# A hybrid decoder layer: output products in two groups of tiles instead of three, key norms in eight columns, chain copies on ScalarE

## The chip, the cores and the metric

The kernel runs on one core of a Trainium2 chip, in one launch. The metric is device time in microseconds of the whole program. TensorE multiplies, VectorE, ScalarE and GpSimd (POOL in the rows) work element by element, SyncE (SP) issues most DMAs. All data are float32.

## The reference, cut to what matters

```python
x = x + 0.5 * swiglu(rms_norm(x, ffn1_norm), ffn1_w_in, ffn1_w_out)     # half step 1
h = rms_norm(x, mix_norm)
p_rwkv, p_q, p_k, p_v, p_gate = split(h @ w_in)
y_a = rwkv7_time_mix(p_rwkv, ...)      # 16 heads of 64, 1024 tokens
y_b = dilated_attention(p_q, p_k, p_v, ...)
x = x + (sigmoid(gate_a) * (y_a @ w_proj_rwkv) + sigmoid(gate_b) * (y_b @ w_proj_attn)) @ w_out
x = x + 0.5 * swiglu(rms_norm(x, ffn2_norm), ffn2_w_in, ffn2_w_out)     # half step 2

def swiglu(h, w_in, w_out):            # D_FF = 2816 = 22 tiles of 128
    gate, up = split(h @ w_in)
    return (silu(gate) * up) @ w_out

# in rwkv7_time_mix
kk = heads(k * k_k)
kk = kk / maximum(sqrt(sum(kk * kk, axis=-1)), 1e-12)
k = k * (1 + (a - 1) * k_a)
wkv = wkv7_scan(r, decay, k, v, -kk, kk * a)    # state = state*w + (state@a) b + v k, out = state@r
```

x is 1024 tokens by 1024 columns; the output has the same shape.

## The kernel before, in words

Every large product is made at float32 quality from three float32r products: each operand is split into a high part (a cast, ScalarE, L74) and a rest (a subtraction, VectorE or GpSimd, L75), and high x high, high x rest and rest x high are summed in PSUM.

**The half steps** (`Ffn`). The activation has 22 row tiles of 128 (called f tiles; 1024 tokens each). Tiles 20 and 21, the last made, stay on the chip and are multiplied with their rows of `w_out` first (`second`, L365). Tiles 0 to 17 were written to memory (`spill`) and are brought back, each together with its rows of `w_out`, as one "raw" tile of 1 MB (`out_raw`, L380, two DMAs). They are multiplied by `Seven`, a scheme with seven block products in place of eight for a 2x2 split: a pair of f tiles gives the operands, `prep` (L104) splits the two operands of one step and makes sums in place on GpSimd, `step` (L129) issues the 12 products of one step into four PSUM tiles. `kk` is the number of pairs in a group. After the last step of each of the seven products `out_evac` (L399) adds the four PSUM tiles to one or two blocks of x each: ten additions per row of four, 40 in a group. Tiles 18 and 19 (`acts_back`, `out_load`, `out_split`) are fetched in between and multiplied last.

`run` (L426) puts the raw tiles in six slots and six parts of the old activation tile (`fresh`, the tiles hhi and hlo), and six more in the slots when the first group is done. Operands are prepared three steps ahead (`RING`). The two sets of PSUM tiles, `pp` and `po`, are taken in turns.

**The mixing stage** (`Rwkv`). The 1024 tokens of a pair of heads are two units of 512; 16 units run in a staggered way: `prep`, `late`, `solve` and `chain` of four neighbouring units are generators that say at which time they want their next piece (`PT`, `ST`, in units), and `drive` takes the earliest. Dense products of the input projection (L593, `pd`) fill TensorE between them. What the framework then makes of it is the order on each engine.

- `prep` (L817) of a unit squares k (L836), sums the squares over each head by a product with a matrix of ones at split precision (`head_sum`, L808, into PSUM tile `pn`), takes the root (L842), the reciprocal of the 128x512 result (L844), a minimum (L845, GpSimd), and multiplies by k (L861). kk then goes into ta (L868), AL (L873) and BK (L875). r's product with the decays (L859, GpSimd) fills AL's third part.
- `solve` (L953) inverts a triangular matrix by 32x32 products (pt, px) with updates of XX on VectorE between them, and makes the state maps M (L1041 to L1043, VectorE, twelve instructions per unit).
- `chain` (L1045) passes the state through eight chunks: product (L1061), state copy (L1064, ScalarE); after four chunks the outputs are copied to `o` (L1070), alternately by ScalarE and VectorE; then their squares are summed (L1082, L1084).

PSUM tiles tagged `ps` are four, used in turn by all these pieces.

Of the kernel before, what the change touches and what calls it, by code (L numbers as in the profile page):

```python
# [7 lines left out]
F32 = mybir.dt.float32  # L8
# [5 lines left out]
P = 128  # L14
# [67 lines left out]
RING = 3  # L82
H = NT // 2
L, R = slice(0, 512), slice(512, 1024)
GK = 3
NG_OUT = 3
OUT = (0, 1, 5, 2, 4, 3, 6)
MIX = (0, 4, 1, 5, 2, 3, 6)
ADDS = (((1, 0), (1, 3)), ((1, 0),), ((1, 3),), ((1, 3), (-1, 1)), ((1, 3), (-1, 2)), ((1, 1),), ((1, 2),))
# [3 lines left out]
class Seven:  # L93
# [3 lines left out]
    def __init__(self, tc, kk, order, ring, banks, pool_a=(), pool_b=()):  # L97


        self.tc, self.kk, self.order, self.ring, self.banks = tc, kk, order, ring, banks  # L100
        self.pool_a, self.pool_b = pool_a, pool_b
        self.b = []

    def prep(self, j, n, k, lo, hi):  # L104

# [23 lines left out]
    def step(self, n, k, evac):  # L129

        nc, last = self.tc.nc, self.kk - 1
        if k == 0:
            pool, tag = self.banks(n)
            self.po = [pool.tile([P, 512], F32, tag=tag, name=tag, bufs=4) for _ in range(H)]
        ah, al, bh, bl = self.b.pop(0)
        for i, po in enumerate(self.po):
            t = slice(i * P, (i + 1) * P)
            nc.tensor.matmul(po, ah[:, t], bh, start=k == 0, stop=False)  # L138
            nc.tensor.matmul(po, ah[:, t], bl, start=False, stop=False)  # L139
            nc.tensor.matmul(po, al[:, t], bh, start=False, stop=k == last)  # L140
            if k == last:
                evac(self.order[n], i, po)


class Ffn:
# [245 lines left out]
        return [t.rearrange("p a b -> p (a b)") for t in self.ring()] + [bt[:, 0], bt[:, 1]]  # L391

    def out_prep(self, j):
        if j < 7 * GK * NG_OUT:
            g, n, k = j // (7 * GK), j // GK % 7, j % GK
            f = 2 * GK * g + k
            self.seven.prep(j, n, k, self.raws[f], self.raws[f + GK])

    def out_evac(self, p, i, ps):  # L399
        V, x = self.tc.nc.vector, self.x  # L400
# [24 lines left out]

    def run(self, before, done):  # L426

        first = 2 * GK * NG_OUT
        slots = iter(range(6))
        for j in range(len(FIRST), len(ORDER)):  # L430
            f, n = ORDER[j]
            self.product(j)
            self.prep(j + RING)
            if f >= NF - 2:
                if n == 0:
                    self.out_load(f)
                elif n == 1:
                    self.out_split(f)
            if f == NF - 1 and n in (0, 1, 5):
                for k in range(2):  # L440
                    m = next(slots)
                    self.out_raw(m // 2 + GK * (m % 2), self.slot(m, F32))
        hT = self.fresh(F32)
        parts = [t.rearrange("p k (a t) -> p k a t", a=2).rearrange("p (b k) a t -> p b (k a) t", b=4) for t in hT]
        for m in range(6):
            self.out_raw(2 * GK + m // 2 + GK * (m % 2), parts[m // 4][:, m % 4])
        banks = lambda n: ((self.cx.ps_d, "pp"), (self.cx.ps_o, "po"))[n % 2]
        self.seven = Seven(self.tc, GK, OUT, self.out_ring, banks, POOL_A)
        for j in range(RING):
            self.out_prep(j)  # L450
        self.second((NF - 2, NF - 1), None)
        self.turn_sums(self.tc.nc.vector.tensor_sub)
        per = 7 * GK
        for j in range(per * NG_OUT):
            self.seven.step(j // GK % 7, j % GK, self.out_evac)
            self.out_prep(j + RING)
            if j == per:
                for m in range(6):
                    self.out_raw(4 * GK + m // 2 + GK * (m % 2), self.slot(m, F32))
            for n in range(2):  # L460
                if j == per + 4 + 6 * n:
                    self.acts_back(first + n)
# [28 lines left out]
def rwkv_consts(tc, cx, pool, dram, W):  # L491
# [28 lines left out]
    nc.gpsimd.memset(ce[0:64, 0:64], 1.0)  # L520
    nc.gpsimd.memset(ce[64:128, 64:128], 1.0)
    nc.vector.tensor_copy(new("bones_r", [P, P], F32R), ce)

    nc.vector.scalar_tensor_tensor(ce, ce, -1.0 / C, cx.ident, ALU.mult, ALU.add)

# [247 lines left out]
class Rwkv:  # L773
# [43 lines left out]
    def prep(self, n):  # L817
# [16 lines left out]
        k = q.k[:, ts_]  # L834
        sq = new("sq", [P, HS])
        nc.scalar.activation(sq, k, AF.Square, scale=col("k_k"))  # L836
        hi = new("sh", [P, HS], 1, F32R)
        V.tensor_copy(hi, sq)
        pn = cx.ps_s.tile([P, 512], F32, tag="ps", name="pn")
        self.head_sum(pn, (sq, hi))  # L840
        kk = new("kk", [P, HS])
        nc.scalar.activation(kk, pn, AF.Sqrt)  # L842
        yield T + PT[1] + 0.03
        V.reciprocal(kk, kk)  # L844
        G.tensor_scalar(kk, kk, 1e12, None, ALU.min)  # L845
        V.tensor_tensor_scan(tw, K["reset"], tw, 0.0, ALU.mult, ALU.add)
        yield T + PT[2]
        lam = new("lam", [P, HC, C + 1])
# [7 lines left out]
        r = q.r[:, ts_]  # L856

        u.AL = AL = new("AL", [P, HC, 3, C], 2)
        G.tensor_mul(AL[:, :, 2], ch(r), lam[:, :, 1:C + 1])  # L859
        yield T + PT[2] + 0.07  # L860
        V.scalar_tensor_tensor(kk, k, col("k_k"), kk, ALU.mult, ALU.mult)  # L861
        yield T + PT[2] + 0.10
        u.k2 = k2 = new("k2", [P, HS], 2)
        V.tensor_scalar(k2, ta, col("k_a"), col("c1"), ALU.mult, ALU.add)
# [3 lines left out]
        V.tensor_mul(ta, ta, kk)  # L868
        BK = u.BK = new("BK", [P, HC, 2, C])
        tt = PT[3]  # L870
        for b, h in enumerate((E, O)):
            yield T + tt
            V.scalar_tensor_tensor(AL[h, :, b], ch(kk)[h], -1.0, lam[h, :, 0:C], ALU.mult, ALU.mult)  # L873
# [171 lines left out]
    def chain(self, n):  # L1045
# [8 lines left out]
        for c in range(HC):  # L1054
# [10 lines left out]
            if i == 3:  # L1065

                for par, dst in enumerate((E, O)):
                    for e, src in enumerate((O, E)):
                        k = slice(c - 3 + e, c + 1, 2)
                        (V.tensor_copy if e else nc.scalar.copy)(o[dst, k], pc[src, par:4:2, e])  # L1070
            yield n + (c + 1) / 8

        p = n // 2
# [661 lines left out]
```

## Time and profile before

| | |
|---|---|
| time, median of 3 runs | 2981.69 us (2977.22 to 2982.45) |
| the profiled execution's own time | 2981.99 us |
| its span | 2980.3 us |
| TensorE busy | 2807.6 us (94%) |
| VectorE busy | 2121.5 us (71%) |
| ScalarE busy | 1262.5 us (42%) |
| GpSimd busy | 1165.5 us (39%) |
| mean granted TensorE clock | 0.987 of 2.4 GHz |

The span runs from the first to the last instruction that the profiler saw; the time has 1.7 us more around it. A busy share is a mean over stages with different limits. The first half step lies in 0 to 725 us, attention to 1183, the RWKV part to about 2010, the merge to 2300, the second half step to the end.

### The profile page before, as it was taken

How to read it: one execution, taken by the hardware profiler on the slowest of the kernel's cores; microseconds unless marked ns; L12 is line 12 of the kernel's file. 1: busy time of each engine (PE TensorE's matmuls, PEld its weight loads, DVE VectorE, ACT ScalarE, POOL GpSimd, SP SyncE). 2: the span in 40 equal slices, each digit the busy share in tenths (PEclk: the TensorE clock that was granted, in tenths of full speed). 3: DMA queues.
4: the chain of work that ended last, by engine and by line, in shares of the span. 5: the costliest groups of instructions: out<-in, count | busy, mean ns of one | idle time of the engine just before them, and what ended most of it. 6: DMA issues, size and time to landing. Idle time of an engine off the chain costs nothing.

```text
span 2980.3 us, 56827 instructions
## 1 busy us (share of the span) xinstructions
PE 2807.6 (94%) x23406; PEld 2232.7 (75%) x23406; DVE 2121.5 (71%) x2924; ACT 1262.5 (42%) x2418; POOL 1165.5 (39%) x1017
## 2 busy tenths in 40 slices
PE   7999998898999999999999998999878999999899
PEld 5888887677667778787778777877666888887677
DVE  7676678998565764767675767442899766678998
ACT  5332232334556663455545555452335332332332
POOL 3333234663101112443434344315775233334653
PEclk9999999999999999999999999999999999999999
DMA  3222225203431124111121111139320122225201
GB/s 113 72 85 82 82 86 197 99 1 90 138 106 36 31 78 125 53 51 45 45 63 47 47 42 52 48 115 307 117 64 22 64 82 82 85 84 213 106 1 57
DMA packets 252244, 246.72 MB, mean 83 GB/s; under 512 B 26288, under 2 KB 192336, under 8 KB 251984
## 3 DMA queue, kind: packets, MB, share of 16 engines
q1 hardware_dynamic: 250832, 238.89, 24.7%
q8 instruction: 184, 3.01, 0.4%
q10 hardware_dynamic: 1152, 4.19, 0.4%
q14 instruction: 76, 0.62, 0.1%
HBM read 181.03 MB, written 62.01 MB: 82 GB/s over the span
## 4 chain that ended last, share of the span: by engine, by line
PE 69%; DVE 21%; issue 4%; DMA 3%; ACT 2%; SPq 0%; POOL 0%; DVEq 0%; ACTq 0%; POOLq 0%
PE pp L282 25%; PE pd L593 22%; DVE bl L75 2%; DVE ob L75 2%; DVE x L403 2%; PE pp L139 2%; PE pp L140 1%; PE pp L138 1%; PE plm L897 1%; PE pc L1061 1%; PE pt L973 1%; PE pl L760 1%; PE px L984 1%; DVE alo L75 1%; PE pz L1019 1%
## 5 line engine op out<-in xcount | busy, mean ns | idle before, releaser
L593 PE MATMUL pd<-hhi,whi 128*128 128x512 f32 (+1 forms) x1064 | 430.6, 405 | 3.8 <-DVE gb L1584 2.2
L593 PE MATMUL pd<-hlo,whi 128*128 128x512 f32 (+1 forms) x1064 | 433.0, 407 | 0.0
L593 PE MATMUL pd<-hhi,wlo 128*128 128x512 f32 (+1 forms) x1064 | 428.8, 403 | 0.6 <-POOL wlo L574 0.6
L574 POOL TENSOR_TENSOR wlo<-raw,whi 128x1024 fp32r<-128x1024 f32 (+2 forms) x69 | 160.8, 2331 | 454.5 <-ACT whi L573 395.2
L282 PE MATMUL pp<-e,bh 128*128 128x512 f32 x1056 | 335.4, 398 | 3.1 <-ACT bh L74 2.5
L253 POOL TENSOR_TENSOR rg<-ru,rg 128x512 f32<-128x512 f32 x44 | 58.1, 1321 | 584.2 <-DVE bl L75 584.2
L282 PE MATMUL pp<-hhi,bl 128*128 128x512 f32 x704 | 277.1, 394 | 2.3 <-DVE bl L75 2.3
L282 PE MATMUL pp<-hhi,bh 128*128 128x512 f32 x704 | 278.0, 395 | 0.0
L282 PE MATMUL pp<-hlo,bh 128*128 128x512 f32 x704 | 276.5, 393 | 0.0
L74 ACT CAST bh<-rg 128x512 fp32r<-128x512 f32 x176 | 105.3, 620 | 331.9 <-PE pp L282 167.8
L593 PEld LDWEIGHTS pd<-hhi,whi 128*128 128x128 f32 (+1 forms) x1064 | 199.6, 188 | 51.3 <-issue 4.6
L282 PEld LDWEIGHTS pp<-e,bh 128*128 128x128 f32 x1056 | 199.0, 189 | 51.7 <-ACT bh L74 3.3
L593 PEld LDWEIGHTS pd<-hlo,whi 128*128 128x128 f32 (+1 forms) x1064 | 199.6, 188 | 48.4 <-issue 5.0
L593 PEld LDWEIGHTS pd<-hhi,wlo 128*128 128x128 f32 (+1 forms) x1064 | 199.7, 188 | 46.3 <-issue 4.2
L282 PE MATMUL pp<-e,bl 128*128 128x512 f32 x528 | 210.0, 398 | 0.0
L75 DVE TENSOR_TENSOR bl<-rg,bh 128x512 fp32r<-128x512 f32 x176 | 156.6, 890 | 73.3 <-ACT bh L74 73.3
L306 DVE TENSOR_TENSOR sg<-sg,pp 128x512 f32<-128x512 f32 x162 | 110.5, 682 | 102.9 <-PE pp L282 102.8
L282 PEld LDWEIGHTS pp<-hhi,bl 128*128 128x128 f32 x704 | 132.7, 189 | 33.4 <-DVE bl L75 3.1
L282 PEld LDWEIGHTS pp<-hlo,bh 128*128 128x128 f32 x704 | 132.8, 189 | 30.0
L282 PEld LDWEIGHTS pp<-hhi,bh 128*128 128x128 f32 x704 | 132.7, 188 | 29.4
L1064 ACT ACTIVATE SV<-pc,lamC 64x64 f32<-64x64 f32 x240 | 73.8, 308 | 116.7 <-PE pc L1061 114.8
L74 ACT CAST bh<-e 128x512 fp32r<-128x512 f32 x84 | 52.1, 620 | 166.5 <-PE pp L139 98.2
(483 smaller groups left out, 6788.7 us busy)
## 6 DMA issues: line engine op xcount, KB each, us to landing
raw<-in_w_in_dram SPq DMA_DIRECT2D x60, 512.0 KB
rg<-in_ffn_w_in_dram SPq DMA_DIRECT2D x44, 512.0 KB
ru<-in_ffn_w_in_dram SPq DMA_DIRECT2D x44, 512.0 KB
act_d<-spill SPq DMA_DIRECT2D x80, 256.0 KB
e<-act_d SPq DMA_DIRECT2D x24, 512.0 KB
e<-in_ffn_w_out_dram SPq DMA_DIRECT2D x24, 512.0 KB
gt_d<-gate SPq DMA_DIRECT2D x32, 256.0 KB
x<-in_x_dram SPq DMA_DIRECT2D x8, 512.0 KB
```

What stands on the lines that cost most here:

```text
L74: nc.scalar.copy(hi, src)
L75: (eng or nc.vector).tensor_sub(lo, src, f32(hi))
L138: nc.tensor.matmul(po, ah[:, t], bh, start=k == 0, stop=False)
L139: nc.tensor.matmul(po, ah[:, t], bl, start=False, stop=False)
L140: nc.tensor.matmul(po, al[:, t], bh, start=False, stop=k == last)
L253: G.tensor_sub(b11, b12, b11)
L282: nc.tensor.matmul(ps, a[:, k], b[:, k], start=m == 0, stop=m == 11)
L306: add = lambda o, a: V.tensor_add(o, a, ps)
L403: (V.tensor_add if sign > 0 else V.tensor_sub)(q, q, ps)
L574: (nc.gpsimd if self.pool_lo else nc.vector).tensor_sub(wlo[:, :kd, :n], raw[:, :kd, :n], f32(whi[:, :kd, :n]))
L593: nc.tensor.matmul(ps[:n], a[:, k, :n], b[:, k, t], start=i == 0, stop=i == 3 * kd - 1)
L1064: nc.scalar.activation(nxt[h, e], pc[h, i, e], AF.Copy, scale=lam[h, c])
```

## The change

It has four parts. (1) The 18 f tiles of the output product form two groups, of five and of four pairs, instead of three groups of three pairs; the first ten raw tiles go to six slots and four parts of the old activation tile, the next four to its other four parts, the last four to slots that come free while the first group's last product is prepared. PSUM tiles are taken in turns through all products of both groups. (2) The squares of k are summed per head by four products whose stationary operand is the 128x128 block of squares and whose moving operand has two columns (`heads`), so that the norms of 128 tokens by eight columns result; root, maximum and reciprocal work on 128x8; GpSimd spreads the result to 128x512, TensorE transposes it back into a PSUM tile `pk`, and kk's product reads that. (3) r's product is issued later. (4) All copies of the chain's outputs are ScalarE's.

```diff
-GK = 3
-NG_OUT = 3
+GROUPS = (5, 4)
+IN_SEVEN = 2 * sum(GROUPS)
+STEPS = [(g, n, k) for g, kk in enumerate(GROUPS) for n in range(7) for k in range(kk)]
...
         if k == 0:
-            pool, tag = self.banks(n)
+            pool, tag = self.banks(self.done)
+            self.done += 1
...
     def out_prep(self, j):
-        if j < 7 * GK * NG_OUT:
-            g, n, k = j // (7 * GK), j // GK % 7, j % GK
-            f = 2 * GK * g + k
-            self.seven.prep(j, n, k, self.raws[f], self.raws[f + GK])
+        if j < len(STEPS):
+            g, n, k = STEPS[j]
+            lo, hi = self.pair(g, k)
+            self.seven.prep(j, n, k, self.raws[lo], self.raws[hi])
+
+    def pair(self, g, k):
+
+        f = 2 * sum(GROUPS[:g]) + k
+        return f, f + GROUPS[g]
...
-        for m in range(6):
-            self.out_raw(2 * GK + m // 2 + GK * (m % 2), parts[m // 4][:, m % 4])
+        places = iter([parts[m // 4][:, m % 4] for m in range(8)])
+        for f in todo:
+            self.out_raw(f, next(places))
+        todo = iter(order[1])
+        for p in places:
+            self.out_raw(next(todo), p)
...
-        per = 7 * GK
-        for j in range(per * NG_OUT):
-            self.seven.step(j // GK % 7, j % GK, self.out_evac)
+        free = (0, 2, 4, 1)
+        per = 7 * GROUPS[0]
+        for j, (g, n, k) in enumerate(STEPS):
+            self.seven.kk = GROUPS[g]
+            self.seven.step(n, k, self.out_evac)
+
+            m = j + RING - (per - GROUPS[0])
+            if g == 0 and 0 <= m - 1 < len(free):
+                self.out_raw(next(todo), self.slot(free[m - 1], F32))
             self.out_prep(j + RING)
-            if j == per:
-                for m in range(6):
-                    self.out_raw(4 * GK + m // 2 + GK * (m % 2), self.slot(m, F32))
...
+    nc.vector.tensor_copy(new("heads", [P, 2]), ce[:, 0:P:C])
...
         nc.scalar.activation(sq, k, AF.Square, scale=col("k_k"))
-        hi = new("sh", [P, HS], 1, F32R)
-        V.tensor_copy(hi, sq)
+
         pn = cx.ps_s.tile([P, 512], F32, tag="ps", name="pn")
-        self.head_sum(pn, (sq, hi))
+        for c in range(4):
+            nc.tensor.matmul(pn[:, 2 * c:2 * c + 2], sq[:, c * P:(c + 1) * P], K["heads"], start=True, stop=True)
+        nrm = new("nrm", [P, 8])
+        nc.scalar.activation(nrm, pn[:, 0:8], AF.Sqrt)
+        yield T + PT[1] + 0.03
+        V.tensor_scalar(nrm, nrm, 1e-12, None, ALU.max)
+        V.reciprocal(nrm, nrm)
         kk = new("kk", [P, HS])
-        nc.scalar.activation(kk, pn, AF.Sqrt)
-        yield T + PT[1] + 0.03
-        V.reciprocal(kk, kk)
-        G.tensor_scalar(kk, kk, 1e12, None, ALU.min)
+        G.tensor_copy(kk.rearrange("p (a c) -> p a c", c=C), nrm.unsqueeze(2).broadcast_to([P, 8, C]))
...
         u.AL = AL = new("AL", [P, HC, 3, C], 2)
-        G.tensor_mul(AL[:, :, 2], ch(r), lam[:, :, 1:C + 1])
+        pk = cx.ps_s.tile([P, 512], F32, tag="ps", name="pk")
+        for c in range(4):
+            nc.tensor.transpose(pk[:, c * P:(c + 1) * P], kk[:, c * P:(c + 1) * P], cx.ident)
         yield T + PT[2] + 0.07
-        V.scalar_tensor_tensor(kk, k, col("k_k"), kk, ALU.mult, ALU.mult)
+        V.scalar_tensor_tensor(kk, k, col("k_k"), pk, ALU.mult, ALU.mult)
...
         tt = PT[3]
+        yield T + tt
+        G.tensor_mul(AL[:, :, 2], ch(r), lam[:, :, 1:C + 1])
...
-                        (V.tensor_copy if e else nc.scalar.copy)(o[dst, k], pc[src, par:4:2, e])
+                        nc.scalar.copy(o[dst, k], pc[src, par:4:2, e])
```

What it makes of the order, at three places. Line numbers of the changed kernel are its own; behind the change they are up to 24 higher than before.

VectorE in the output product of the first half step, one product's end to the next one's. Before (x are the additions out of PSUM, bl and ob the rests of the two operands of a step):

```order
L403 TENSOR_TENSOR x<-x,pp 128x512 x8
L75 TENSOR_TENSOR bl<-hlo,bh 128x512
L75 TENSOR_TENSOR ob<-hlo,ob 128x512
L75 TENSOR_TENSOR bl<-hhi,bh 128x512
L75 TENSOR_TENSOR ob<-hhi,ob 128x512
L75 TENSOR_TENSOR bl<-hhi,bh 128x512
L75 TENSOR_TENSOR ob<-hhi,ob 128x512
L403 TENSOR_TENSOR x<-x,po 128x512 x4
```

With the change, in the second group:

```order
L411 TENSOR_TENSOR x<-x,po 128x512 x8
L75 TENSOR_TENSOR bl<-e,bh 128x512
L75 TENSOR_TENSOR ob<-e,ob 128x512
L75 TENSOR_TENSOR bl<-e,bh 128x512
L75 TENSOR_TENSOR ob<-e,ob 128x512
L75 TENSOR_TENSOR bl<-hlo,bh 128x512
L75 TENSOR_TENSOR ob<-hlo,ob 128x512
L75 TENSOR_TENSOR bl<-hlo,bh 128x512
L75 TENSOR_TENSOR ob<-hlo,ob 128x512
L411 TENSOR_TENSOR x<-x,pp 128x512 x4
```

Four steps' splits stand between two blocks of additions (five in the first group), where three stood.

SP's queue in the same stage; hlo and e are places of raw tiles (the old activation tile, the slots), vu the loads for tiles 18 and 19. Before:

```order
L384 DMA hlo<-act_d 128x1024
L385 DMA hlo<-in_ffn_w_out_dram 128x1024
L360 DMA vu<-act_d 128x512 x2
L349 DMA vu<-in_ffn_w_out_dram 128x512 x2
L360 DMA vu<-act_d 128x512 x2
L349 DMA vu<-in_ffn_w_out_dram 128x512 x2
L384 DMA e<-act_d 128x1024
L385 DMA e<-in_ffn_w_out_dram 128x1024
```

With the change:

```order
L387 DMA hlo<-act_d 128x1024
L388 DMA hlo<-in_ffn_w_out_dram 128x1024
L387 DMA hlo<-act_d 128x1024
L388 DMA hlo<-in_ffn_w_out_dram 128x1024
L363 DMA vu<-act_d 128x512 x2
L352 DMA vu<-in_ffn_w_out_dram 128x512 x2
L363 DMA vu<-act_d 128x512 x2
L352 DMA vu<-in_ffn_w_out_dram 128x512 x2
L387 DMA e<-act_d 128x1024
L388 DMA e<-in_ffn_w_out_dram 128x1024
```

Four DMAs more stand ahead of vu; the reloads of the slots stay behind it, four tiles instead of six.

VectorE in the unit of the RWKV part that has r's dense product beside it. Before, ahead of the updates of M and behind them:

```order
L844 RECIPROCAL kk<-kk 128x512
L651 SCALAR_TENSOR_TENSOR k<-pd,v_mu,k 128x511
L655 TENSOR_TENSOR k<-k,carry 128x1
L861 SCALAR_TENSOR_TENSOR kk<-k,v_k_k,kk 128x512
L868 TENSOR_TENSOR ta<-ta,kk 128x512
L1070 COPY o<-pc 64x2x64 x2
L1041 TENSOR_TENSOR M<-pm,MB 64x4x128
```

```order
L1043 TENSOR_TENSOR M<-pm,AL 64x4x64
L1084 TENSOR_REDUCE st<-y 128x8
L976 TENSOR_TENSOR B<-pt,mk 128x256
L873 SCALAR_TENSOR_TENSOR AL<-kk,lam 64x8x64
L978 TENSOR_TENSOR XX<-B,eye 128x256
```

With the change, at the same two places:

```order
L862 TENSOR_SCALAR nrm<-nrm 128x8
L863 RECIPROCAL nrm<-nrm 128x8
L669 SCALAR_TENSOR_TENSOR k<-pd,v_mu,k 128x511
L673 TENSOR_TENSOR k<-k,carry 128x1
L1108 TENSOR_REDUCE st<-y 128x8
L1065 TENSOR_TENSOR M<-pm,MB 64x4x128
```

```order
L1067 TENSOR_TENSOR M<-pm,AL 64x4x64
L883 SCALAR_TENSOR_TENSOR kk<-k,v_k_k,pk 128x512
L1000 TENSOR_TENSOR B<-pt,mk 128x256
L890 TENSOR_TENSOR ta<-ta,kk 128x512
L1002 TENSOR_TENSOR XX<-B,eye 128x256
L897 SCALAR_TENSOR_TENSOR AL<-kk,lam 64x8x64
```

The products kk and ta went behind the updates of M, the sum of squares (L1084, now L1108) went ahead of them, and the copies are gone.

## Rows read from the trace of the kernel before

**Rows 1.** The chain that ended last, whole span, by engine.

```profile
PE 69%; DVE 21%; issue 4%; DMA 3%; ACT 2%; SPq 0%; POOL 0%; DVEq 0%; ACTq 0%; POOLq 0%
```

**Rows 2.** Windows: stretch, us; busy (count) PE, PEld, DVE, ACT, POOL; clock, DMA, GB/s.

```profile
503.20:699.80 196.60, 180.77 (x756) 141.37 (x755) 188.27 (x236) 73.41 (x128) 123.81 (x99) 0.99 0.14 42
2756.80:2953.40 196.60, 181.47 (x758) 142.41 (x758) 189.32 (x236) 73.53 (x128) 119.61 (x75) 0.98 0.11 41
2640.00:2690.00 50.00, 50.00 (x218) 40.70 (x217) 35.05 (x43) 14.71 (x26) 17.84 (x12) 1.00 0.28 87
454.00:492.00 38.00, 30.36 (x122) 23.54 (x121) 32.99 (x36) 11.87 (x21) 23.98 (x16) 0.96 0.86 331
```

**Rows 3.** TensorE's waits, 503 to 700 us: us in total, times, longest.

```profile
PE po L139 <- DVE ob L75: 10.8, 10, 3.7
PE pp L139 <- DVE ob L75: 3.2, 4, 1.5
PE pp L138 <- DVE x L403: 1.7, 1, 1.7
```

**Rows 4.** TensorE's waits, 1282 to 1777 us, five pairs of units.

```profile
PE pt L973 <- DVE XX L986: 12.8, 5, 2.6
PE px L984 <- DVE B L976: 10.9, 10, 1.2
```

**Rows 5.** Windows of the roomy and the tight unit of one pair.

```profile
1493.30:1543.20 49.90, 49.80 (x901) 41.15 (x901) 28.86 (x53) 26.71 (x57) 22.22 (x29) 1.00 0.23 66
1543.20:1592.20 49.00, 43.53 (x893) 35.32 (x893) 37.26 (x67) 26.04 (x58) 17.99 (x29) 1.00 0.11 35
```

**Rows 6.** Groups of instructions, VectorE, 505 to 688 us: busy us, mean ns, idle.

```profile
L403 DVE TENSOR_TENSOR x<-x,pp 128x512 f32<-128x512 f32 x68 | 41.5, 675 | 0.0
```

**Rows 7.** Groups of instructions, whole span, VectorE: busy us, mean ns, idle before.

```profile
L844 DVE RECIPROCAL kk<-kk 128x512 f32<-128x512 f32 x16 | 53.6, 3352 | 23.1 <-ACT kk L842 23.1
...
L1070 DVE COPY o<-pc 64x128 f32<-64x128 f32 x64 | 18.2, 284 | 103.0 <-ACT o L1070 102.5
```

**Rows 8.** The chain in 1480 to 1579 us: start, us, what.

```profile
1499.26 0.95 PE pvt L936 x8
...
1508.41 0.44 PE pyt L1093 x4
1508.85 0.39 PE pc L1061 x4
...
1527.81 0.43 PE pn L814
1528.24 0.24 PE pn L815
```

**Rows 9.** VectorE's instructions in order: start, us, what [idle before].

```profile
1512.99 0.69 DVE L951 TENSOR_TENSOR bonus<-pb,v 128x512 f32<-128x512 f32 x1 [2.60 <-PE pb L815]
...
1537.26 0.75 DVE L861 SCALAR_TENSOR_TENSOR kk<-k,v_k_k,kk 128x512 f32<-128x512 f32 x1 [1.47 <-POOL kk L845]
1538.04 0.69 DVE L868 TENSOR_TENSOR ta<-ta,kk 128x512 f32<-128x512 f32 x1
1542.45 0.28 DVE L1070 COPY o<-pc 64x128 f32<-64x128 f32 x1 [3.71 <-ACT o L1070]
...
1543.37 0.69 DVE L1041 TENSOR_TENSOR M<-pm,MB 64x512 f32<-64x512 f32 x1
...
1549.99 0.69 DVE L1084 TENSOR_REDUCE st<-y 128x8 f32<-128x512 f32 x1
...
1568.99 0.28 DVE L1070 COPY o<-pc 64x128 f32<-64x128 f32 x1 [1.95 <-ACT o L1070]
```

**Rows 10.** ScalarE's instructions in order, in the tight unit.

```profile
1543.38 0.63 ACT L1082 ACTIVATE y<-o 128x512 f32<-128x512 f32 x1 [0.35 <-DVE o L1070]
```

**Rows 11.** The chain in 420 to 700 us.

```profile
516.14 0.60 DVE bl L75
...
520.26 1.71 DVE ob L75
```

More of the change, by code (lines that the diff above doesn't have):

```diff
@@ L102, in __init__ @@
         self.b = []
+        self.done = 0
     def prep(self, j, n, k, lo, hi):
@@ L426, in run @@
     def run(self, before, done):
-        first = 2 * GK * NG_OUT
+        first = IN_SEVEN
         slots = iter(range(6))
+        order = [[f for k in range(kk) for f in self.pair(g, k)] for g, kk in enumerate(GROUPS)]
+        todo = iter(order[0])
         for j in range(len(FIRST), len(ORDER)):
@@ L440, in run @@
                 for k in range(2):
-                    m = next(slots)
-                    self.out_raw(m // 2 + GK * (m % 2), self.slot(m, F32))
+                    self.out_raw(next(todo), self.slot(next(slots), F32))
         hT = self.fresh(F32)
         parts = [t.rearrange("p k (a t) -> p k a t", a=2).rearrange("p (b k) a t -> p b (k a) t", b=4) for t in hT]
-        for m in range(6):
-            self.out_raw(2 * GK + m // 2 + GK * (m % 2), parts[m // 4][:, m % 4])
+        places = iter([parts[m // 4][:, m % 4] for m in range(8)])
[4 more added lines that the diff above has]
+            self.out_raw(next(todo), p)
         banks = lambda n: ((self.cx.ps_d, "pp"), (self.cx.ps_o, "po"))[n % 2]
-        self.seven = Seven(self.tc, GK, OUT, self.out_ring, banks, POOL_A)
+        self.seven = Seven(self.tc, GROUPS[0], OUT, self.out_ring, banks, POOL_A)
         for j in range(RING):
```

## The prediction

> **What bounds the kernel now.** I read the whole chain of waits first. TensorE carries most of it and VectorE nearly all the rest [rows 1], so an edit pays only where TensorE stands still, and there the question is what it waits for. So next come the windows of the two stages that the change enters, and TensorE's waits in them.
>
> The first stage is the output product of a feed-forward half step, which stands in the program twice. Both copies last 196.6 us [rows 2]. In a stretch where TensorE never waits, 218 products of 128x512 take 50 us [rows 2], 0.229 us each; the stage's 63 steps have 756 of them, 173.4 us. So 23.2 us of each copy are lost. VectorE is busy 188.3 and 189.3 us of the two [rows 2]: it is the longer engine. TensorE's waits in the first copy, 15.7 us together, all name VectorE [rows 3]: its residual subtractions (L75) and once the additions out of PSUM (L403). The rest of the 23.2 us I put down to products that restart slowly behind a wait; the granted clock is 0.99 there, so little of it is clock.
>
> The second stage is the RWKV part, 16 units. Over five pairs TensorE's solver products wait 23.7 us for VectorE, 4.7 a pair [rows 4]. The two units of a pair are unlike: in one stretch of 49.9 us TensorE is busy 49.8, in the next of 49.0 only 43.5 [rows 5]. I call them the roomy and the tight unit. In the tight one VectorE starts the updates of M at 1543.4 and has no gap before 1567 [rows 9]; that burst is what the solver waits for.
>
> **Fewer groups in the output stage.** Nine pairs of row tiles in two groups (5 and 4) instead of three of 3: the products stay 756, splits and sums per pair stay. What goes is one third of the additions into x: ten per token tile row, four rows, once less, so 40 of 120 additions per copy. One costs 0.675 us alone; in a run 68 of them occupy 41.5 us [rows 6], 0.61 each, so VectorE loses 24.4 us and needs 188.3 - 24.4 = 164 us against TensorE's 173.4. The longest engine becomes TensorE. The order also shows five or four prepared steps between two blocks of additions instead of three, so a block of 8 (4.9 us) has 11 to 13.8 us of products beside it instead of 8.3. Bounds of the gain per copy: 23.2 us if no wait is left; 8 if bunching keeps two thirds of the loss. I take 17, three quarters, since VectorE's demand is 5% under TensorE's but comes in bursts, and eight extra splits still fall in the first group. Two copies: **-34 us**. The banks now alternate across groups too, which removes the wait of 1.7 us for L403 [rows 3]; it is inside the 17.
>
> What could eat this is the loads. Ten tiles of 1 MB must now be there for the first group, four of them in the old activation tile, used from the fourth step. The queues moved 331 GB/s in the stretch that fetches them [rows 2], so two tiles more than before are some 6 us of transfer, and the first steps lie behind the 22 us of products of the last two row tiles: hidden. SP issues four DMAs more ahead of the loads that the spare row tiles wait for; same cover. The last four tiles go to slots that come free when the first group's last product is prepared, seven steps (19 us) before they are read: at that rate 4 MB take 13 us. Cost nothing, with 6 us of cover left.
>
> **Key norms in eight columns.** VectorE loses a reciprocal of 3.35 us per unit [rows 7] and a cast, GpSimd a subtraction; ScalarE's root shrinks. But that reciprocal stands where VectorE waits on both sides of it: right before the tight burst it still waits 3.7 us [rows 9]. So on the path it is worth only what the first unit shows, where nothing runs beside it: **-2 us**. TensorE gives two products (0.43 + 0.24 us on the chain [rows 8]) for four products with a full weight load and two columns, and four transposes. No row has two columns; the nearest with the same weights and type is the state product, two in 0.39 us [rows 8], so four are 0.78 us; above, four of 128 columns take 0.95 [rows 8], below, nothing. Four transposes take 0.44 us [rows 8]. Net 0.78 + 0.44 - 0.67 = +0.55 us a unit (-0.23 to +0.72).
>
> The Trainium skill (TensorE: Matmul & The Clock Gate, Part 4: PE-mode transpose) gives about 275 ns for a transpose of 128x128 within a kernel. By it four would cost 1.1 us, the 16 units 10.6 us more, and the sum below would be 2964; the row here, at float32 and pipelined, says 0.11 each, and I go by the row.
>
> In the roomy units TensorE has no slack, so 8 x 0.55 = **+4.4 us**. In the tight units VectorE decides. There the order moves the product kk and the product ta (0.75 and 0.69 us, before at 1537.3, in a gap [rows 9]) behind the last update of M, because kk now reads the transposes in PSUM. Against that the sum of squares (0.69 us [rows 9]) moves from behind the updates to before them, where it has to wait for ScalarE's copies and square (square at 1543.4 to 1544.0 [rows 10]): the updates start about 1.2 us later. One more PSUM tile per unit in a rotation of four also makes the next solver product wait for the last update instead of the one before it; that shifts TensorE by up to 1.7 us, but into time in which it waits now. Together 0 to +1.2 us a tight unit; I take 0.4, 8 x 0.4 = **+3 us**. Full bounds of the RWKV stage: -44 us (all of 8 x 4.7 gone, no new weight loads, the first unit) to +15 us (8 x 0.72 + 8 x 1.2).
>
> **Copies and r's product.** VectorE gives its two copies of 0.28 us per half unit to ScalarE; they alternate with ScalarE's own, and VectorE waits for each (103 us in all [rows 7]). On ScalarE four in a row end when the fourth ends now. The wait is freed in gaps, in the tight unit the updates wait for TensorE's products until then anyway: nothing. r's product on GpSimd stands later by a sixteenth of a unit; GpSimd sat before it waiting for the last update anyway: nothing.
>
> **The sum.** -34 - 2 + 4.4 + 3 = -28.6. Made against the profiled execution's 2981.99 us (span 2980.3 and 1.7 around it; 0.3 us above the median of the three runs, 2981.69): **2953 us**.
>
> **The rivals.** *The burst dissolves* (10%). VectorE is relieved by some 5 us a unit and TensorE's 4.7 us a pair go: 38 us less, 9 us of new TensorE work, 2 of the first unit: -31 instead of +5, 2917 us. For it: all those waits name VectorE. Against: what is taken off lies outside the burst. *The output stage stays bunched* (10%). A residual subtraction takes 0.60 us alone and 1.7 us when it meets GpSimd [rows 11]; GpSimd's 124 us of work are the same in a shorter stage, so more may be hit. At 1.09 on average the 108 subtractions are 118 us; at 1.25 they are 17 more, which eats most of the 24: gain 5 a copy, 2977 us. The rule behind it is in the Trainium skill (SBUF — State Buffer, SBUF: two separate sides): VectorE with two SBUF inputs and GpSimd exclude each other for a whole instruction. *Slower* (5%): VectorE's queue now waits, at kk, for TensorE's transposes, which wait for a bank that VectorE frees; behind kk stand ta, both halves of AL and BK of the unit, and the solver's first product. If the full sum of the pieces comes on the path in every unit (0.75 + 0.69 + 1.2 + 1.7 = 4.3 us), it costs 69 us and the result is 3015 us. It decides above 2.1 us a unit, where it overtakes the 34. For it: VectorE's burst has no gap; against: in the roomy unit it has one of 2.6 us soon after [rows 9]. *The late reload* (3%), where the change does not do what it says: if the second group's tiles come 10 us late in both copies, 2973 us.
>
> **How the numbers follow.** Forecast 2953 with 72%; its own bounds are 2939 (23 a copy) to 2974 (10 a copy, RWKV +12). Leaving out the dissolved burst and part of the bunched stage, 8 in 10 lie in **2934 to 2974**. What a measurement can tell from no change is 0.2%, 6 us. Faster: the forecast, the dissolved burst, the late reload and a third of the bunched stage, 88%. Same: the rest of that, 7%. Slower: 5%.
>
> **What would show it.** Right: 80 additions instead of 120 in each copy, the copies at 176 to 184 us, TensorE's waits for VectorE there under 6 us; in the RWKV stage a pair of 99 to 101 us with waits of TensorE still 4 to 6 us, now behind an M update or kk; copies only on ScalarE. Wrong: output copies over 190 us, mean subtractions above 1.2 us, GpSimd or ScalarE waiting for a load in the second group's first steps; or pairs under 97 or over 103 us.

## The result, and the profile after

| | before | changed |
|---|---|---|
| time, median | 2981.53 us (4 runs, 2977.22 to 2982.45) | 2997.43 us (4 runs, 2996.12 to 3003.26) |
| ratio | | 1.0062, 95% interval 1.005 to 1.0074 |
| the profiled execution: time, span | 2981.99, 2980.3 us | 3003.26, 3001.5 us |
| TensorE busy | 2807.6 us | 2841.4 us |
| VectorE busy | 2121.5 us | 2002.8 us |
| mean granted TensorE clock | 0.987 | 0.981 |

The change is slower by 0.62%, 15.9 us; the forecast was 2953, with a range of 2934 to 2974. VectorE lost 119 us of work, and TensorE got 34 us more. (The profiled execution is the slowest of the four; the ledger further down is made from one at the median.)

**The output copies.** Windows of the two copies of the changed kernel (columns as in [rows 2]):

```profile
500.90:692.60 191.70, 181.07 (x757) 143.03 (x755) 169.43 (x204) 72.70 (x128) 122.28 (x99) 0.98 0.12 34
2783.80:2974.50 190.70, 179.71 (x757) 143.19 (x756) 169.37 (x197) 72.73 (x128) 117.15 (x75) 0.98 0.09 31
```

They were 196.6 us [rows 2] and lost 5 and 6. VectorE has fallen to 169 us (the prediction had 164), under TensorE's 173.4, and TensorE still waits. Its waits in the first copy, 501 to 695 us:

```profile
PE pp L142 <- DVE ob L75: 7.3, 7, 2.0
PE po L142 <- DVE ob L75: 3.4, 4, 2.0
PE po L376 <- DVE om L528: 1.0, 1, 1.0
```

Of 14.0 us that named the subtractions [rows 3] 10.7 are left; the wait for an addition, 1.7 us, is gone. Four of these waits, 1.6 to 2.0 us long, hold 7.6 of the 10.7 us, and three of the four end between 541 and 557 us. What VectorE does just then, and GpSimd beside it, shows in the timelines of both engines from 536 us on:

```profile
537.58 1.77 DVE L75 TENSOR_TENSOR bl<-hhi,bh 128x512 fp32r<-128x512 f32 x1
539.28 1.75 DVE L75 TENSOR_TENSOR ob<-hhi,ob 128x512 fp32r<-128x512 f32 x1
540.95 1.77 DVE L75 TENSOR_TENSOR olo<-vu,ohi 128x512 fp32r<-128x512 f32 x1
```

```profile
537.07 1.74 POOL L129 TENSOR_TENSOR e<-e 128x512 f32<-128x512 f32 x1
538.77 1.71 POOL L124 TENSOR_TENSOR e<-e 128x512 f32<-128x512 f32 x1
540.55 1.61 POOL L127 TENSOR_TENSOR e<-e 128x512 f32<-128x512 f32 x1
```

The two run in step: one subtraction for each of GpSimd's sums in place, each as long as the sum, where alone it takes 0.60 us [rows 11]. From 534 to 555 us no addition stands between them.

**The RWKV part.** Windows of a roomy and a tight unit, halves of one pair:

```profile
1500.70:1551.40 50.70, 50.70 (x904) 41.34 (x902) 23.18 (x46) 27.23 (x61) 19.36 (x28) 1.00 0.23 64
1551.40:1602.10 50.70, 46.42 (x914) 37.81 (x914) 34.31 (x67) 27.23 (x64) 16.93 (x29) 0.97 0.11 34
```

A pair took 98.9 us [rows 5] and now takes 101.4. VectorE has much more air than before, and the pair is longer. TensorE's waits over five pairs (1282 to 1789 us):

```profile
PE pt L997 <- DVE XX L1010: 9.7, 5, 2.4
PE px L1008 <- DVE B L1000: 7.3, 9, 1.9
PE pbt L950 <- DVE M L1067: 5.8, 10, 0.9
PE pk L881 <- DVE M L1067: 2.0, 5, 0.4
```

24.8 us stand where 23.7 stood [rows 4]: the solver's waits (pt and px) went down by 7, and two new ones for the PSUM tile of an update of M came. So waits are not where the time went. TensorE's timeline around the new products:

```profile
1483.49 1.05 PE L858 MATMUL pn<-heads,sq 128*128 128x2 f32 x8
1484.41 0.48 PE L611 MATMUL pd<-hhi,whi 128*128 128x512 f32 x1
...
1553.06 0.63 PE L881 MATMUL pk<-ident,kk 128*128 128x128 f32 x4 [0.39 <-DVE M L1067]
1553.45 0.48 PE L611 MATMUL pd<-hlo,whi 128*128 128x512 f32 x1
```

From start to next start the four norm products (eight passes, each with its weights) hold TensorE 0.92 us and the four transposes 0.39; the sum had 0.78 and 0.44.

**Two things that the prediction had no term for.** First the windows of 30 us behind attention in which TensorE has dense products alone, of the kernel before and of the changed one:

```profile
1135.00:1165.00 30.00, 30.00 (x134) 24.82 (x134) 12.36 (x15) 6.88 (x10) 7.23 (x4) 1.00 0.60 178
```

```profile
1135.00:1165.00 30.00, 30.00 (x130) 24.12 (x129) 9.54 (x12) 6.06 (x8) 7.58 (x8) 1.00 0.77 209
```

Without a wait, at a full clock, it does four products fewer. Taken from the starts of the rows in this stretch, the mean step from one dense product to the next is 226.7 ns before and 233.3 now. Second the granted clock. In the changed kernel it falls behind nearly every tight unit (window, then TensorE's timeline inside it):

```profile
1470.00:1480.00 10.00, 10.00 (x230) 7.94 (x230) 3.97 (x9) 5.51 (x14) 3.70 (x7) 0.66 0.08 30
```

```profile
1475.79 0.63 PE L611 MATMUL pd<-hlo,whi 128*128 128x512 f32 x1
1476.21 0.63 PE L611 MATMUL pd<-hhi,wlo 128*128 128x512 f32 x1
1476.64 0.63 PE L611 MATMUL pd<-hhi,whi 128*128 128x512 f32 x1
```

The dense products come every 0.43 us there: the clock is at 1.2 of its two levels, 1.2 and 2.4 GHz. Ahead of it TensorE had been busy 65% over 10 us. In the kernel before the same trough (62%) left the clock at 1.00. The windows of the changed kernel and of the kernel before:

```profile
1460.00:1470.00 10.00, 6.53 (x189) 4.95 (x182) 9.85 (x15) 4.50 (x10) 5.88 (x4) 1.00 0.42 133
```

```profile
1460.00:1470.00 10.00, 6.22 (x223) 5.09 (x222) 8.07 (x14) 4.66 (x9) 4.04 (x3) 1.00 0.43 133
```

### The profile page after: what moved, and what is told of

Its sections match the earlier page's. It is cut to its first block, busy times and chain, and to the rows that moved or that the text cites. A ratio compares the mean times of both kernels' runs of the same rounds, so it can differ in the third digit from the quotient of the medians.

```text
span 3001.5 us, 56989 instructions
## 1 busy us (share of the span) xinstructions
PE 2841.4 (95%) x23566; PEld 2256.1 (75%) x23566; DVE 2002.8 (67%) x2781; ACT 1268.5 (42%) x2480; POOL 1129.3 (38%) x1001
## 5 line engine op out<-in xcount | busy, mean ns | idle before, releaser
L611 PE MATMUL pd<-hhi,whi 128*128 128x512 f32 (+1 forms) x1064 | 436.9, 411 | 7.6 <-DVE gb L1608 3.2
L611 PE MATMUL pd<-hhi,wlo 128*128 128x512 f32 (+1 forms) x1064 | 437.7, 411 | 0.6 <-POOL wlo L592 0.6
L591 ACT CAST whi<-raw 128x1024 fp32r<-128x1024 f32 (+2 forms) x69 | 69.9, 1013 | 126.6 <-PE pd L611 71.3
```

The costliest lines, as they stand in the source:

```text
L591: nc.scalar.copy(whi[:, :kd, :n], raw[:, :kd, :n])
L611: nc.tensor.matmul(ps[:n], a[:, k, :n], b[:, k, t], start=i == 0, stop=i == 3 * kd - 1)
```

## The experiments

Times are medians. Each is compared with runs of the kernel before on its own chip (2980.9 to 2982.2 us); differences below are to those. "Clock loss" of a stretch is worked out from windows of 10 us: TensorE's busy time times what the granted clock lacks to 1.

### The four parts, one at a time

The first part alone (b1); the last part alone (b2); all but the norms (a3); the new norms alone (a4, `heads` 64 bytes wide).

```diff
 b2:
-  (V.tensor_copy if e else nc.scalar.copy)(o[dst, k], pc[src, par:4:2, e])
+  nc.scalar.copy(o[dst, k], pc[src, par:4:2, e])
 a3 (the changed kernel without its second part):
-  for c in range(4):
-      nc.tensor.matmul(pn[:, 2 * c:2 * c + 2], sq[...], K["heads"], ...)
+  self.head_sum(pn, (sq, hi))
...
```

b1: 

> The kernel before with the first part alone: groups of five and four pairs in both half steps; norms, copies and r's product as before. By the trace of the changed kernel an output copy takes 191.3 and 190.3 us instead of 196.5 and 196.0, so 11 us less in all: 2968 to 2972. By the prediction's term (17 a copy): 2947. If the gain in the copies is given back behind them (a fall of the granted clock, a later mixing stage): 2978 to 2982.

b2: 

> The kernel before with the last part alone: all copies of the chain's outputs on ScalarE. Prediction's term: nothing, 2981 within 2 us. Rival (ScalarE's queue then holds the state copies of the chain back, and the chain's tail, which nothing covers, grows): 3 to 7 us more, 2984 to 2988, with the last product of the state later and the mixing stage 1330 to 1334 us instead of 1327.

a3: 

> The changed kernel without its second part: key norms as before (two products with the matrix of ones, reciprocal of 128x512), no `heads`, no transposes; groups of five and four pairs, the later product of r and the copies on ScalarE stay. The two output copies gain 5 us each by the trace of the changed kernel. If the whole loss comes with the norms (their place or their products): 2968 to 2974. If the copies on ScalarE cost too, as the chain's tail in the changed kernel suggests (5 us longer in its last 40 us): 2976 to 2982.

a4: 

> The kernel before with the new norms alone (`heads` 16 columns wide, so that whi and wlo stay at multiples of 64 bytes); three groups, the copies on both engines and r's product stay as before. Theory 'norms': the products cost 0.91 + 0.40 us a unit where 0.57 went, 12 us over 16 units, and the clock's falls come on top: 2994 to 3004. Theory 'place': the products alone, less what VectorE gets back in the tight units: 2984 to 2994.

| | median, us | ratio, 95% interval | to before, us |
|---|---|---|---|
| b1 groups alone | 2967.03 | 0.9955 (0.9942 to 0.9968) | -14.3 |
| b2 copies alone | 2987.30 | 1.0023 (1.0014 to 1.0032) | +6.0 |
| a3 all but the norms | 2972.58 | 0.9975 (0.9966 to 0.9984) | -8.3 |
| a4 new norms alone | 3006.87 | 1.0089 (1.0076 to 1.0103) | +26.0 |

Groups and copies give -14.3 + 6.0 = -8.3, which is a3: r's product costs nothing that the intervals show. (a3 came out in the branch that gives the norms the whole loss, but only because the groups gave 14.3 and not the 10 in it: the copies cost 6.0.) Of b1's 14.3 the two copies show 10.5 (191.2 and 191.5 us). The norms are the loss, and a4 lies above both of its branches. The prediction had the chain's copies free, and they are not; b2 lies in the branch of its rival. In the mixing stage of b2 only the tail is longer, 84 us for 77 from TensorE's last product for a state map (pm) to the end. There ScalarE is all that the chain has. ScalarE's timeline of b2 and of the kernel before at the first half of the last unit:

```profile
2008.65 0.64 ACT L1064 ACTIVATE SV<-pc,lamC 64x64 f32<-64x64 f32 x2
2009.32 1.07 ACT L1070 COPY o<-pc 64x128 f32<-64x128 f32 x4
2010.40 0.63 ACT L1064 ACTIVATE SV<-pc,lamC 64x64 f32<-64x64 f32 x2
```

```profile
2008.17 0.64 ACT L1064 ACTIVATE SV<-pc,lamC 64x64 f32<-64x64 f32 x2
2008.84 0.26 ACT L1070 COPY o<-pc 64x128 f32<-64x128 f32 x1
2009.54 0.63 ACT L1064 ACTIVATE SV<-pc,lamC 64x64 f32<-64x64 f32 x2 [0.44 <-PE pc L1061]
```

One copy stood between two state copies, now four do; the next state copy starts 1.75 us behind the one before it instead of 1.37. That is little; but a fall of the clock follows (0.66 over 2010 to 2030 us, where before has 1.00), and the tail's dense products take 5.1 us longer. The mixing stage's other parts are unchanged within 1 us. That the copies bring this fall is argued from one profile: in a second profile of the kernel before the clock falls at the same place too, for 3.4 us where b2 has 13.6, and the tail is 79 us. Over all executions b2's granted clock is the lower one, 0.982 on the mean of eleven against 0.986 of eighteen.

### Where the tiles lie

The build places tiles one below the other; `heads` (8 bytes, 32 with its padding) moves everything allocated behind it. The dense products' moving tiles, hhi and hlo, stay where they are. The weight tiles of the mixing stage:

```
             whi (first)   wlo (first)
before       208064        216256
changed      208032        216224
```

a1 adds to the kernel before only the line that makes `heads`; a2 and c1 make `heads` 64 and 128 bytes wide, in the changed kernel and in a4.

```diff
 a1:
+    nc.vector.tensor_copy(new("heads", [P, 2]), ce[:, 0:P:C])
 a2, a4 ([P, 32] in c1):
-    nc.vector.tensor_copy(new("heads", [P, 2]), ce[:, 0:P:C])
+    nc.vector.tensor_copy(new("heads", [P, 16])[:, 0:2], ce[:, 0:P:C])
```

a1: 

> The kernel before, with one more constant tile of 128x2 that is filled and never read (the line that fills `heads`, alone). Nothing else changes; the tile takes 32 bytes a partition, and the weight tiles whi and wlo of the mixing stage, before at multiples of 64 bytes, then lie 32 bytes lower, as they do in the changed kernel. Theory 'place' (a dense product takes longer when its stationary operand lies at an odd multiple of 32 bytes): in the stretch after attention, where dense products stand alone, they follow each other every 0.233 us instead of 0.227; over the stage the difference is 2.7 ns on the mean of 3192 products, so 8 to 12 us more, 2990 to 2994. Theory 'norms' (the loss is the small products of the norms, and the clock that falls beside them): 2981 within 3 us, spacing 0.227.

a2: 

> The changed kernel with `heads` made 16 columns wide, of which two are used: 64 bytes instead of 32, so that whi and wlo are back at multiples of 64 bytes. Theory 'place': dense spacing of the mixing stage back at 0.227 where nothing else runs, 8 to 12 us less than the changed kernel, 2985 to 2989. Theory 'norms': 2997 within 3 us.

c1: 

> The kernel before with the new norms alone, `heads` 32 columns wide (128 bytes), so that whi and wlo lie at odd multiples of 64 bytes as in the kernel before; with 64 bytes they lay at multiples of 128, and dense products that stand alone then came every 0.229 us instead of 0.227. Theory 'place' (all of the weights' address counts): 2 to 5 us less than with 64 bytes (3007 there), 3002 to 3005. Theory 'norms': 3007 within 3 us.

a1 took 2986.88 us, 1.0020 (1.0012 to 1.0029): +6.0 us for a tile that nothing reads, between the two branches. Its window beside those above:

```profile
1135.00:1165.00 30.00, 30.00 (x130) 24.12 (x129) 9.98 (x15) 7.47 (x11) 5.95 (x3) 1.00 0.67 168
```

130 products, as in the changed kernel, 233.3 ns apart. Over the mixing stage a1's dense products take 12 to 13 us more than in two profiles of the kernel before, and TensorE's waits are 7 to 9 us shorter. a2 took 2993.85 us, 1.0047 (1.0033 to 1.0061): 2.9 us less than the changed kernel, against its own runs of before (13.0 for 15.9). Its step is 228.9 ns, not 226.7: part of the way back, and the intervals overlap. c1 took 3007.89 us, 1.0103 (1.0085 to 1.0120): no gain over a4, and its window shows why:

```profile
1135.00:1165.00 30.00, 30.00 (x131) 24.12 (x130) 12.15 (x15) 6.68 (x9) 7.25 (x4) 1.00 0.63 178
```

233.3 ns again, with whi at 207936, a multiple of 64 like 208064. So my rule of odd multiples of 32 has fallen. What stands is the effect: kernels with whi at 208064 have 226.6 to 226.9 ns (before, its second profile, a3, b1 to b4, c4, d1, d2), at 208000 228.9 (a2, a4), at 208032 233.3 to 233.4 (a1, changed, its second profile), at 207936 233.3 to 233.4 (c1, c2, c3): eighteen profiles, and the number follows the place each time. What about the address decides it stays open (wlo and other tiles move with whi). It is worth 3 to 6 of the 15.9 us, by a2 and by a1; the 3 are not clear of noise.

### What the norms cost

c2 is c1 with the norm products issued twice, c3 is c1 without transposes and their tile.

```diff
 c2:
-        for c in range(4):
+        for c in (0, 1, 2, 3) * 2:
             nc.tensor.matmul(pn[:, 2 * c:2 * c + 2], ...)
 c3:
-        pk = cx.ps_s.tile([P, 512], F32, tag="ps", name="pk")
-        for c in range(4):
-            nc.tensor.transpose(pk[...], kk[...], cx.ident)
-        V.scalar_tensor_tensor(kk, k, col("k_k"), pk, ALU.mult, ALU.mult)
+        V.scalar_tensor_tensor(kk, k, col("k_k"), kk, ALU.mult, ALU.mult)
```

c2: 

> As the run before this one, with the four norm products of a unit issued twice (the second time over the same result). It prices them on the path: they take 0.91 us a unit in the trace, 14.5 us over 16 units. If TensorE is the bound in roomy and tight units alike: 12 to 17 us more than the run before. If the tight units hide them (the prediction's view of the waits): 6 to 9 us. If they also bring on falls of the granted clock: above 17 us.

c3: 

> As the first run of this call, without the four transposes of a unit and their PSUM tile: kk's product reads what GpSimd spread, before it is turned (so the norms of other tokens and channels are used). It prices the transposes with the PSUM tile that they take from the solver's rotation. Transposes alone: 0.36 us x 16 = 6 us less. If the wait of the next solver product for the PSUM tile of the updates of M is on the path too (9 us in the trace of the changed kernel): 12 to 16 us less.

c2 took 3036.00 us, 28.1 more than c1: the upper branch. In its trace the products hold TensorE 15.9 us longer, and the clock loss of 1190 to 2120 us goes from 16.1 to 25.3: 9.2 more. Nothing is hidden in the tight units. c3 took 2995.87 us, 12.0 less than c1, the edge of its upper branch: 6.4 are the transposes on TensorE, 2.5 clock loss. The waits that its branch named are not the reason, since TensorE waits 48.2 us in c3's mixing stage and 47.2 in c1's; the rest I can't place.

So in c2 15.9 us of TensorE's work cost 28.1, and the clock has part in it. The 9.2 us come from one profile of each kernel; over all executions the granted clock is 0.978 on the mean of c2's four and 0.982 of c1's six. Whether the falls belong to a kernel or to one execution, second profiles of both kernels were to tell:

before: 

> The kernel before, for a second profile. If the falls of the granted clock belong to the kernel: 5 to 9 us lost to them in the mixing stage (6.5 in the first profile), none behind most tight units. If to the execution: some other number, up to the 13 to 22 of the kernels with the new norms.

changed: 

> The changed kernel, for a second profile. If the falls of the granted clock belong to the kernel: 17 to 25 us lost to them in the mixing stage (21.6 in the first profile), behind nearly every tight unit. If to the execution: some other number, down to the 6.5 of the kernel before.

The clock loss from 1190 us to the end of the mixing stage was 6.5 and 7.4 us before, 21.6 and 15.8 with the change (under the 17 expected): it varies with the execution, and in these four the kernels stay apart. But it does not belong to the new norms alone. By the same working a3 and b2, with the norms as before, lose 17.5 and 12.0 us, and a1, with nothing but the unread tile, 10.9, with a fall behind five tight units in a row (1366 to 1762 us). From a3 to a2, the step that puts the new norms in, the loss grows by 2.4 us only. What brings a fall behind a tight unit stays open. The second profiles' executions (2981.56 and 2997.34 us) lie at the medians of their kernels, so the ledger is made from them:

| stretch, by TensorE's products | before, us | changed, us | |
|---|---|---|---|
| to the first output copy | 501.9 | 503.5 | +1.7 |
| first copy to the first dense product of the mixing stage | 243.9 | 237.6 | -6.2 |
| mixing stage, first to last dense product | 1326.0 | 1352.8 | +26.9 |
| to the second output copy | 684.5 | 684.0 | -0.5 |
| second copy to the last product | 218.9 | 212.9 | -6.0 |

In the mixing stage (each product's time taken from its start to the next start, less the wait) norm products and transposes minus the old ones make +12.8 us, the dense products +17.5. The clock loss over the whole stage grew by 5.6 (from 10.2 to 15.8); the other 12 I put down to their place, which is argued (a1, where only the place changed, has 12 to 13, 2 to 3 of them clock loss). Waits and the solver's other products make up the difference, -3.

### What holds the output copies

b3 leaves out the additions of the second group, b4 GpSimd's sums; c4 moves the sums to VectorE beside two groups, d1 beside three.

```diff
 b3 (out_evac):
+        self.evacs = getattr(self, 'evacs', 0) + 1
+        if 28 < self.evacs <= 56:
+            return
 b4 (prep, ahead of the sums):
+        if self.order is OUT:
+            return
 c4 (on b1) and d1 (on the kernel before), at the same place:
+        if self.order is OUT:
+            G = nc.vector
```

b3: 

> The kernel before, still with three groups, but the 40 additions into x after the second group are left out in both half steps (so a third of the output product does not reach x). It takes from VectorE what the two groups take from it, and nothing else changes. If VectorE's total load bounds the output copy, as the prediction had it: 17 us less a copy, 2947. If the copy is held by the few steps in which the operands' subtractions meet GpSimd's sums, additions elsewhere do not matter: 2 to 5 us less a copy, 2971 to 2977.

b4: 

> The kernel before, with GpSimd's eight sums in place per pair of row tiles left out in the output product of both half steps (the block products then multiply unsummed operands); all 120 additions and all subtractions stay. If the subtractions that meet these sums (1.7 us instead of 0.6) are what TensorE waits for: waits of TensorE fall from 15.7 to under 5 us a copy, the copy to 180 to 185 us, 2957 to 2967. If VectorE's load as such bounds it: less than 5 us a copy, above 2971.

c4: 

> The kernel before with groups of five and four pairs (2967), and GpSimd's sums in place of the output product moved to VectorE. Without the sums VectorE's 108 subtractions took 0.75 us instead of 1.09 on the mean, 37 us less a copy; 72 sums at 0.61 us put 44 us back, so VectorE's load is about what it was, but nothing meets GpSimd any more. If the meeting is what TensorE waits for: 180 to 186 us a copy, 2947 to 2960. If VectorE's load bounds the burst, since sums and subtractions of the same steps now stand in one queue: 2967 to 2985.

d1: 

> The kernel before with its three groups and 120 additions a copy, GpSimd's sums of the output product moved to VectorE. VectorE then has 188 - 37 (subtractions that meet nothing) + 44 (72 sums) = 195 us of work a copy, with two groups 167. If VectorE's load counts as soon as nothing meets GpSimd: the copy stays at 190 to 197 us, 2970 to 2982. If only the meeting counted: 176 to 182 us, 2940 to 2952.

| | median, us | ratio, 95% interval | to before, us |
|---|---|---|---|
| b3 40 additions less | 2971.24 | 0.9965 (0.9955 to 0.9975) | -10.1 |
| b4 no sums | 2927.37 | 0.9818 (0.9804 to 0.9832) | -53.9 |
| c4 two groups, sums on VectorE | 2928.56 | 0.9823 (0.9810 to 0.9836) | -53.7 |
| d1 three groups, sums on VectorE | 2947.83 | 0.9887 (0.9870 to 0.9903) | -33.9 |

b3 is the prediction's 24 us of VectorE per copy, taken off alone: the copies are 193.0 and 194.0 us instead of 196.6, and the time is 10 us less, where 34 were forecast. VectorE's load is then 168 us in a copy of 193:

```profile
501.90:694.90 193.00, 180.89 (x757) 142.99 (x756) 167.96 (x196) 73.30 (x128) 123.69 (x99) 0.98 0.15 42
```

b4 has all 120 additions, and the copies are at TensorE's floor, better than either branch had it; so is c4. (Of b4's 53.9 us the two copies show 43.4; the rest stands mostly in the stretches ahead of them.) Windows of the copies in b4, then d1, then c4, and of the first copy in b1, which is c4 with the sums on GpSimd:

```profile
495.40:671.10 175.70, 175.70 (x757) 141.56 (x756) 151.01 (x236) 72.89 (x128) 29.64 (x42) 1.00 0.16 47
2718.90:2893.00 174.10, 173.93 (x757) 141.51 (x756) 151.05 (x236) 72.97 (x128) 24.28 (x18) 1.00 0.13 46
```

```profile
496.40:679.70 183.30, 177.59 (x755) 142.34 (x754) 182.04 (x295) 72.94 (x128) 31.46 (x42) 0.99 0.15 46
```

```profile
498.10:674.60 176.50, 175.25 (x757) 141.53 (x755) 167.10 (x265) 72.72 (x128) 34.39 (x42) 1.00 0.14 42
2725.70:2901.20 175.50, 173.85 (x757) 141.63 (x756) 167.14 (x258) 72.69 (x128) 29.46 (x18) 1.00 0.10 35
```

```profile
502.60:693.80 191.20, 181.51 (x757) 142.93 (x755) 170.07 (x203) 72.69 (x128) 122.92 (x99) 0.98 0.12 34
```

With the sums on its own queue VectorE does more instructions (265 for b1's 203) in less time (167 us for 170), since its subtractions no longer last as long as GpSimd's sums. A group of them in the first copy, in the changed kernel and in c4:

```profile
L75 DVE TENSOR_TENSOR ob<-e,ob 128x512 fp32r<-128x512 f32 x32 | 37.9, 1187 | 2.0 <-ACT ob L74 2.0
```

```profile
L75 DVE TENSOR_TENSOR ob<-e,ob 128x512 fp32r<-128x512 f32 x32 | 24.8, 776 | 0.1
```

The Trainium skill (SBUF — State Buffer, SBUF: two separate sides) says that VectorE with two SBUF inputs and GpSimd hold a shared port pair in turn, each for a whole instruction; these rows and the steps above agree. d1 tells the causes apart. Its time lies in the branch of the meeting, its copies (183.3 and 182.6 us) just above that branch: the meeting is worth 13 to 14 us a copy with three groups. Once it is gone VectorE's load is the next bound (182 us in a copy of 183, not the 195 that I had worked out), and only then do two groups count by their load, 7 us a copy. Of the versions that leave nothing out c4 is the best here: 1.8% under the kernel before.

On that version d2 moves the chain's copies the other way:

```diff
-  (V.tensor_copy if e else nc.scalar.copy)(o[dst, k], pc[src, par:4:2, e])
+  V.tensor_copy(o[dst, k], pc[src, par:4:2, e])
```

> Two groups with the sums on VectorE (2928.6), and all copies of the chain's outputs on VectorE, the opposite of the change's last part. If copies on ScalarE cost because the state copies of the chain stand behind them: 2 to 6 us less, 2923 to 2927, and the last state product earlier. If two engines side by side is what is good (four copies end when two on each end): 2 to 8 us more.

2931.09 us, 0.9828 (0.9814 to 0.9843), 2.5 us above c4 with overlapping intervals: in the branch for two engines by number, but not clear of no change. Taking the copies off ScalarE gains nothing, so queueing behind copies there is not a steady cost; in b2 the loss shows in the tail.

## Why the prediction was wrong, point by point

- **"VectorE's load bounds the output copy; 17 of its 23 us a copy go."** This step failed, by 11 to 12 us a copy; two groups alone gave 14.3 us, not 34 (b1). The load argument compared totals over 196 us. The waits lie in a few steps, where each subtraction waits out one of GpSimd's sums, and an addition elsewhere gives them little (b3: 3 to 4; the change: 5 and 6). What holds the copy is the meeting of VectorE's subtractions with GpSimd's sums (b4, c4, d1): with the sums on VectorE the copies of the two groups fall from 191 to 176 us, and VectorE's load only from 170 to 167. The rival *the output stage stays bunched* had the size, 5 a copy, and cited the right lock, but not the mechanism: it needed the mean subtraction to rise from 1.09 to 1.25 us, and it stayed (1.08 and 1.09 us over the 102 subtractions of bl and ob on VectorE in the first copy; the eight of tiles 18 and 19 alone grew, by 3.2 us together).
- **"TensorE gets 0.55 us a unit."** Measured 12.8 us over 16 units in the second profiles, 0.80 a unit (0.75 from a3 to a2): above the 0.72 that bounded it. The norm products were 0.92 for 0.78 estimated from the state product, the transposes 0.36 to 0.4 for 0.44, and the two products that they replaced 0.56 for 0.67. For the transposes I went by the row and not by the Trainium skill (TensorE: Matmul & The Clock Gate, Part 4: PE-mode transpose), and both were right: one lasts 273 ns in the new trace, as the page has it, but the next starts 0.1 us after it.
- **"Norms +5.4 us in all, since tight units hide most and the first unit gains 2."** Failed: 21.3 (from a3 to a2). Nothing is hidden in the tight units (c2), the stretch up to the first state product, where I had a gain of 2, is 4 to 5 us longer (a4 against the kernel before, a2 against a3), and two things had no term at all. Of the 18.4 us by which a2's mixing stage is longer than a3's, 12.0 are the products and transposes and 6.0 the dense products, whose place changed with the norms (226.7 to 228.9 ns); the clock loss grew by 1.3. Added to the kernel before by themselves (a4) the norms cost 26.0, with some 6 us of clock loss in it. That TensorE's waits stay at 4 to 6 us a pair was right (5.0), but 17 of the 24.8 us still wait for XX and B, 7.8 for an update of M and none for kk. VectorE's relief gave nothing, as forecast.
- **"Copies: nothing."** Failed by 6.0 us (b2). The argument held in the units; the tail, where the chain alone sets the time, was not looked at, and b2 is longer there.
- **"r's product: nothing", "loads: nothing."** Right as far as the runs tell: -8.3 in a3 is groups and copies alone, within intervals of about 3 us each way, and none of TensorE's waits in the copies names a load.
- **What was missing.** The place of the weight tiles, +3 to +6 us, from an 8-byte constant, and the falls of the clock.
- **The rival that ended slower** (3015) wanted VectorE to wait for the transposes: 4.4 us in the whole trace, not 2.1 a unit. The result was slower by another mechanism than the one priced.

By the runs: -14.3 (groups) + 6.0 (copies) + 21.3 (norms) + 2.9 (place) = +15.9 us. The terms are steps in this order: the 21.3 hold part of the place, and the 2.9 are not clear of noise.

## What to carry to other kernels

Work taken off a busy engine is worth what it frees in the very steps that wait: find those in the timeline, and see which other engine's instruction starts and ends with the slow one, before comparing totals. Small products that replace elementwise work are paid in full where TensorE is the bound, and more than once where its clock falls with them (28.1 us for 15.9 in c2). After any new constant compare the step between products in a stretch that should not have changed.

## What the hardware showed that was not expected

- The step between dense products of 128x512 went by where their weight tiles lie: 226.7, 228.9 or 233.3 ns for four places within 128 bytes; in all eighteen profiles each place has its own step. An 8-byte tile that nothing reads cost 6.0 us (3.6 to 8.6 by the interval).
- The clock fell to 1.2 GHz behind the waits of nearly every tight unit in some kernels, and behind one or two only in others with waits much alike; the clock loss from 1190 us to the end of the mixing stage ranged from 4.5 us (b1) to 25.3 (c2).
- 72 sums a copy on GpSimd cost VectorE about as much time as doing them itself (170 us with them on GpSimd in b1, 167 with them on its own queue in c4).
